# A batched matrix product on one core: the turns of loads and stores in its one DMA queue get unequal lengths

## The chip, the cores and the metric

The kernel runs on one core of a Trainium2 chip. The metric is device time in microseconds (us) of one execution; below it stands beside the span that the profile shows, which is about 1.8 us shorter. DMA is the moving of data between the chip's main memory (HBM) and the core's own. A transfer is issued when SyncE puts it in the queue, and has landed when the last of its 16 records in the trace, one for each DMA engine, is there.

## The reference

Sixteen independent products. Each takes x of 768 x 512 and y of 768 x 1024, both float32, and gives 512 x 1024 in float32:

```python
batch, m, k, n = 16, 512, 768, 1024
def reference(x, y):
    return np.einsum('bkm,bkn->bmn', x, y).astype(np.float32)
```

Per batch 1.57 MB of x and 3.15 MB of y are read, and 2.10 MB are written. I call x and y of one batch a pair. In all, 75.5 MB are read and 33.6 MB written.

## The kernel before

Every transfer is issued by the SyncE sequencer, into one queue, in the order of this program. Each load goes to one of two float32 buffers; VectorE casts it to bf16 (a 16-bit float); TensorE multiplies into PSUM, the memory for its results; ScalarE copies the result to one of five output buffers, which a store then empties.

```python
FIRST = 8
TURN = 4
NO = 5                                  # output buffers
...
def store(b):                           # may it be issued? not before the next batch's matmuls are done
    if b < B - 2:
        nc.sync.wait_ge(groups, 2 * (b + 2))
    else:
        nc.sync.wait_ge(outs, b - (B - 3))
    nc.sync.dma_start(o_v[b], ob[b % NO][:]).then_inc(so[b % NO], 16)

def load(b):                            # the buffer is free when the batch two before has been cast
    i = b % 2
    if b >= 2:
        nc.sync.wait_ge(cast, nx[b - 2])
    wide_dma("x", xs[i][:], x_v[b], 4, True).then_inc(sx[i], 16)
    ...
    wide_dma("y", ys[i][:], y_v[b], 2, True).then_inc(sy[i], 16)

for b in range(B):
    load(b)
    if b + 1 >= FIRST and (b + 1 - FIRST) % TURN == 0:
        a = b + 1 - FIRST
        for c in range(a, a + TURN):
            store(c)
for b in range(B - FIRST + TURN, B - 1):
    store(b)
...
for b in range(B):                      # ScalarE
    if b >= NO:
        nc.scalar.wait_ge(so[b % NO], 16 * (b // NO))     # the store from this buffer has landed
    ...
for b in range(B - NO, B - 2):          # SyncE, before the last store
    nc.sync.wait_ge(so[b % NO], 16 * (b // NO + 1))
...
nc.sync.dma_start(o_v[B - 1], ob[(B - 1) % NO][:])
```

So the queue holds 8 pairs, 4 stores, 4 pairs, 4 stores, 4 pairs, 8 stores. I call each such run a turn, and the passage from one to the next a switch.

## Time and profile before

| | before |
|---|---|
| time, median of the first 3 runs | 260.7 us |
| span of the profiled run | 258.8 us |
| busy: TensorE, VectorE, ScalarE | 70%, 32%, 24% |
| DMA queue, share of 16 engines | 98.6% |
| ScalarE waiting for stores | 60.1 us |

Busy shares of engines are means over the span, so a low share doesn't say that an engine is never waited for.

### The profile page before, as it was taken

Reading aid. Unit: us, or ns where it says so; the run is one execution under the profiler, and the core shown is the slowest. Engines: PE = TensorE matmul, PEld = TensorE weight load, DVE = VectorE, ACT = ScalarE, POOL = GpSimd, SP = SyncE. Lnnn points to the kernel's source line nnn. Section 1 sums busy time; section 2 is a strip of 40 time slices with the busy share of each in tenths; the row PEclk is TensorE's granted clock in tenths of the full one; section 3 lists DMA queues with packets and bytes.
Section 4 is the critical chain, followed back from the end, with each engine's and each line's share of the span. In section 5 each row is a group of like instructions: output and inputs, shape, how many; then the busy total and the mean of one; then the engine's idle time right before and its main releaser. Section 6 shows DMA issues by size and latency. Waiting matters only on the chain. (4 is left out here: it accounts for less than half of the span.)

```text
span 258.8 us, 2506 instructions
## 1 busy us (share of the span) xinstructions
PE 181.6 (70%) x768; PEld 89.3 (34%) x768; DVE 82.0 (32%) x33; ACT 60.9 (24%) x33; POOL 0.2 (0%) x4
## 2 busy tenths in 40 slices
PE   0009999999999006999499920899669980099950
PEld 0004555554545002454145500355325530035520
DVE  0261645527164350011734525002255262300000
ACT  1000442234220005222214002324402200413430
POOL 0000000000000000000000000000000000000000
PEclk9999999999999855899779985699979995569995
DMA  7999989899999999999999989999899999999987
GB/s 273 424 475 410 471 380 479 372 479 395 456 410 441 387 418 430 466 446 418 433 433 425 471 352 443 420 461 479 372 479 403 448 410 390 433 438 420 436 357 324
DMA packets 4514, 109.07 MB, mean 421 GB/s; under 512 B 768, under 2 KB 768, under 8 KB 768
## 3 DMA queue, kind: packets, MB, share of 16 engines
q1 hardware_dynamic: 4512, 109.05, 98.6%
q14 instruction: 2, 0.02, 0.0%
HBM read 75.50 MB, written 33.55 MB: 421 GB/s over the span
## 5 line engine op out<-in xcount | busy, mean ns | idle before, releaser
L157 PE MATMUL ps<-yb,xb 128*128 x768 | 181.6, 402 | 68.0 <-PEq L152 68.0
L157 PEld LDWEIGHTS ps<-yb,xb 128*128 x768 | 89.3, 116 | 159.8 <-issue 89.8
L173 ACT COPY ob<-ps 128x2048 f32<-128x2048 f32 x32 | 59.6, 1872 | 185.3 <-PE ps L157 125.2
L135 DVE CAST yb<-ys 128x6144 bf16<-128x6144 f32 (+1 forms) x17 | 53.8, 3172 | 77.8 <-DMA ys<-in_y_dram 77.8
L131 DVE CAST xb<-xs 128x3072 bf16<-128x3072 f32 x16 | 28.2, 1761 | 62.5 <-DMA xs<-in_x_dram 48.7
L173 ACT ACT_TABLE_LOAD x1 | 1.3, 1283 | 5.3 <-issue 5.3
L203 POOL MEMSET const-bfloat16-1.0<- 128x1 bf16 x1 | 0.1, 103 | 0.0
L203 POOL MEMSET const-uint8-127<- 128x1 uint8 x1 | 0.1, 102 | 0.0
L203 POOL MEMSET const-float32-0.0<- 128x1 f32 x1 | 0.1, 100 | 0.2 <-issue 0.2
L203 POOL MEMSET const-float32-1.0<- 128x1 f32 x1 | 0.1, 99 | 0.0
## 6 DMA issues: line engine op xcount, KB each, us to landing
ys<-in_y_dram SPq DMA_DIRECT2D x16, 3072.0 KB, 18.6
out_dram<-ob SPq DMA_DIRECT2D x16, 2048.0 KB, 27.2
xs<-in_x_dram SPq DMA_DIRECT2D x16, 1536.0 KB, 20.1
```

Source lines behind the costliest of these rows:

```text
L131: nc.vector.tensor_copy(xb[:, i], xs[i][:]).then_inc(cast, 1)
L135: nc.vector.tensor_copy(yb[:, i, ks], ys[i][:, ks]).then_inc(cast, 1)
L157: mm = nc.tensor.matmul(ps[g][:, m, nt], x_w[:, bass.ds(s, 1), kt, mo], yb[:, bass.ds(s, 1), kt, nt * NF:(nt + 1) * NF], start=(kt == 0), ...
L173: cp = nc.scalar.copy(ob[b % NO][:, g * HB:(g + 1) * HB].rearrange("p m (t f) -> p m t f", f=NF), ps[g][:])
L203: nc = _bacc.Bacc("TRN2", target_bir_lowering=False, num_devices=1)
```

## The change

The intent: let output buffers come free before ScalarE asks for them, and shorten the run of stores at the end, without changing how often the queue goes from loads to stores.

```diff
-    FIRST = 8
-    TURN = 4
+    TURNS = [(8, 5), (4, 4), (4, 7)]
...
-    for b in range(B):
-        load(b)
-        if b + 1 >= FIRST and (b + 1 - FIRST) % TURN == 0:
-            a = b + 1 - FIRST
-            for c in range(a, a + TURN):
-                store(c)
-    for b in range(B - FIRST + TURN, B - 1):
-        store(b)
+    loads, stores = iter(range(B)), iter(range(B - 1))
+    for nl, ns in TURNS:
+        for b in islice(loads, nl):
+            load(b)
+        for b in islice(stores, ns):
+            store(b)
```

The third turn takes stores 9 to 14; the last store, of batch 15, follows it, which makes seven.

More of the change, by code (lines that the diff above doesn't have):

```diff
@@ L6 @@
 from contextlib import ExitStack
+from itertools import islice
 import concourse.bass as bass
```

## The prediction

> **What bounds the kernel now.** I read the page from the top. Part 1 shows that no engine is near full: the tensor engine is busy for 70% of the span, the vector engine for 32%, the scalar engine for 24%. Parts 2 and 3 show what is full.
>
> ```profile
> span 258.8 us, 2506 instructions
> PE 181.6 (70%) x768; PEld 89.3 (34%) x768; DVE 82.0 (32%) x33; ACT 60.9 (24%) x33; POOL 0.2 (0%) x4
> ...
> DMA  7999989899999999999999989999899999999987
> ...
> q1 hardware_dynamic: 4512, 109.05, 98.6%
> ...
> HBM read 75.50 MB, written 33.55 MB: 421 GB/s over the span
> ```
>
> The reader is to see that one DMA queue carries every byte, and that its packets fill 98.6% of the time of all 16 engines. The small remainder lies at the two ends: in the stretches from the span's start, nothing moves before 1 us, and nothing after 257 us.
>
> The page's chain that ended last covers only 10% of the span (matmuls, then one copy), because it stops at an instruction whose releaser it cannot follow. So I do not take it as the bound. I go to the order of time on the vector engine, where each cast of y begins when its load lands.
>
> ```profile
> 80.94 3.36 DVE L135 CAST yb<-ys 128x6144 bf16<-128x6144 f32 x1 [5.47 <-DMA ys<-in_y_dram]
> 84.70 1.76 DVE L131 CAST xb<-xs 128x3072 bf16<-128x3072 f32 x1 [0.40 <-DMA xs<-in_x_dram]
> 92.12 3.36 DVE L135 CAST yb<-ys 128x6144 bf16<-128x6144 f32 x1 [5.66 <-DMA ys<-in_y_dram]
> 115.34 1.76 DVE L131 CAST xb<-xs 128x3072 bf16<-128x3072 f32 x1 [19.86 <-DMA xs<-in_x_dram]
> 122.58 3.36 DVE L135 CAST yb<-ys 128x6144 bf16<-128x6144 f32 x1 [5.48 <-DMA ys<-in_y_dram]
> 133.58 3.36 DVE L135 CAST yb<-ys 128x6144 bf16<-128x6144 f32 x1 [5.48 <-DMA ys<-in_y_dram]
> ```
>
> Within a turn of loads, y lands every 11.0 us (133.58 - 122.58), whatever the engines do. I call x and y of one batch, 4.72 MB, a pair: 4.72 MB in 11.0 us is 429 GB/s. Between y of batch 7 (92.12) and y of batch 8 (122.58) lie four stores and one pair: 30.46 - 11.0 = 19.46 us, so 4.87 us for a store of 2.10 MB, or 431 GB/s. A switch between loads and stores is included in that, and stores in the last turn, where there is no switch back, take the same.
>
> The scalar engine shows the same from the other side: its copy into a used output buffer waits for the store from it.
>
> ```profile
> 97.00 3.64 ACT L173 COPY ob<-ps 128x2048 f32<-128x2048 f32 x2 [21.69 <-DMA out_dram<-ob]
> 160.43 3.64 ACT L173 COPY ob<-ps 128x2048 f32<-128x2048 f32 x2 [18.55 <-DMA out_dram<-ob]
> 223.74 3.63 ACT L173 COPY ob<-ps 128x2048 f32<-128x2048 f32 x2 [19.83 <-DMA out_dram<-ob]
> ```
>
> These are stores 0, 4 and 8, each the first of its turn, landing 4.88, 4.88 and 4.89 us after the last y of the turn before it (92.12, 155.55, 218.85). The first store after a switch costs no more than any other. Adding up: first y lands at 14.98; 15 pairs at 11.0 are 165.0; 16 stores at 4.87 are 77.9; together 257.9. The last issue, at 251.67, takes 6.3 us to land, which is 258.0. The time is the sum of the transfers, in any order, with nothing left over.
>
> [...] y of batch 7 is issued at 73.35, and lands at 92.12, in the order of its issue. [...] after an idle stretch the granted clock was 0.50 from 89 to 105 us, and 96 matmuls took 23.85 us. I take 13.4 us for a batch begun cold (10.4 plus about 3) and 10.5 for a warm one; both are estimates from these rows.
>
> **The change part by part.** Instructions on the four compute engines are the same in kind, number and order; only the DMA-issuing engine has another order. It **removes** no transfer and **adds** none. It **moves** store 4 from the head of the second turn of stores to the end of the first, and store 8 from the head of the third to the end of the second. The numbers of switches are unchanged: three from loads to stores, two back. By the sums above the direct cost is 0 us.
>
> What else it could change is whether the queue runs dry. I worked through the new order with the durations above.
>
> Turn 1. Y of batch 7 lands at 92.1, and stores 0 to 4 at 97.0, 101.9, 106.7, 111.6, 116.5. Store 4 is issued when batch 5's matmuls are done (84.4: 73.84 + 10.55), and loads 8 follow at once, the casts that they wait for ending at 75.5 and 84.3. The queue then holds 8 us of load and 24 us of stores, so this wait of the issuer is hidden.
>
> Turn 2. X and y of batch 8 land at 120.2 and 127.4; y of 9, 10, 11 at 138.4, 149.4, 160.4. Batch 8 runs cold from 130.8 to 144.2, batch 9 to 154.6, batch 10 to about 165. Store 8 has to wait for batch 9, so it and loads 12 behind it are issued at about 155, when the queue still holds the rest of pair 11 and three stores (5.4 + 14.6 = 20 us). Hidden. Stores 5 to 8 land at 165.3 to 179.9.
>
> Turn 3. Y of 12 to 15 lands at 190.9, 201.9, 212.9 and 223.9, later than before by one store (5 us); the last stores are then 7 instead of 8, so 5 us are given back exactly. Batch 14's matmuls end at about 228.5; its copy waits for store 9 (228.7) and ends at 232.4; batch 15 runs from 230.8 to some 241 to 244; its last copy ends by about 246, where before it ended at 251.48 (249.61 + 1.87). So the **compute tail** is 5 us earlier. That is the intent, I think: output buffers come free before they are asked for, and the scalar engine's wait for stores falls from 60.1 us to about 22 + 5 + 4 = 31.
>
> What does that buy at the end? Before, the last store was issued only at 251.67.
>
> ```profile
> 250.00:251.50 1.50, 0.00 (x0) 0.00 (x0) 0.00 (x0) 1.48 (x1) 0.00 (x0) 1.00 0.72 306
> 251.50:253.00 1.50, 0.00 (x0) 0.00 (x0) 0.00 (x0) 0.00 (x0) 0.00 (x0) 0.65 0.46 197
> 253.00:257.00 4.00, 0.00 (x0) 0.00 (x0) 0.00 (x0) 0.00 (x0) 0.00 (x0) 0.50 1.08 459
> ```
>
> The columns at the end are granted clock, DMA share and GB/s. The missing shares are 0.28 x 1.5 + 0.54 x 1.5 = 1.23 us of the mean engine: a real hole. But the end is set by the slowest of the 16, not by the mean. Store 14, issued at 241.18, took 11.8 us to landing, thus 253.0; the last one landed at 258.0. That is 5.0 us apart against 4.87 for a store without a hole, so the slowest engine lost only about 0.15 us; the others idled because they had finished their shares early. After the change the last store is held only until store 13 lands (a wait on its semaphore precedes it; 253.0 - 4.9 = about 248), is issued near 248.3, and the hole closes. **Sum:** 0 for transfers, -0.15 for the hole, so 260.7 - 0.15 = about 260.5 us.
>
> **Rivals.** First, **the whole hole counts**: if all engines had been equally late, closing it gives 1.2 us, about 259.5. For it: 1.23 us is really missing. Against it: the 5.0 us between the last two landings. Still within 2%. Second, **long bursts of stores are slower**, or a switch from five stores back to loads costs more: each 1% on a store is 0.05 us, and 16 stores give 0.8 us, about 261.4. Against it: in the kernel before, stores run eight in a row at the end at the same 4.87. Third, **a new wait starves the queue**: store 4 or store 8 blocks the issuer while it waits for matmuls, and the loads behind it are held. If the tensor engine were 20 us later in turn 2 than I find, the queue would run dry by that excess; 5 us of it would make 265.5. Against it: a reserve of 20 us at the tighter place. Fourth, **the compute wait was the bound**: a reader of part 1 who sees 125.2 us of waiting on ACT and 68 us of idle PE may expect 5 us from the earlier compute tail, about 255.7. Against it: the transfers alone add up to 257.9 of 258.8.
>
> **Range and chances.** The centre is 260.5. The lower edge, 259.6, takes in most of the first rival; the upper one, 261.3, takes in the second and a few tenths of difference between chips (the three runs of before span 0.34 us). 2% is 5.2 us, so faster would need the fourth rival and slower the third: 1% and 2%.
>
> **What would show it.** Right: DMA share again near 98.6% or a little above; y of batch 8 landing at about 127.4 and of batch 15 at about 223.9; ACT's wait for stores near 31 us in place of 60.1; the last copy ending by about 246; the last store issued near 248 and no stretch with a share under 0.7 between 250 and 254; the span within 0.5 us of 258.8. Wrong: a hole in the DMA share in the stretches 115 to 125, 155 to 185 or 218 to 230, stores of over 4.95 us in the runs of five or seven, or a last store that is still issued after 251 us.

The clock and the 23.85 us are measured. The rates of 429 and 431 GB/s are measured, but that they leave no room was not shown. That only an empty queue costs time was the assumption. The 13.4 us for a cold batch is an estimate from the trace: two batches of 48 matmuls took 23.85 us, less 10.5 for the second.

## The result

The changed kernel took 260.72 us (median of 4 runs, 260.52 to 260.85); the kernel before, in 4 runs, 260.6 (260.4 to 260.74). The ratio is 1.0004, with a 95% interval from 0.9987 to 1.0022: no difference. The profiled span was 259.0 us, and each instruction kept its place on the four compute engines.

From the page of the changed kernel, in the order of the lines shown for the kernel before:

```profile
span 259.0 us, 2506 instructions
PE 179.0 (69%) x768; PEld 88.9 (34%) x768; DVE 82.0 (32%) x33; ACT 60.9 (24%) x33; POOL 0.2 (0%) x4
...
DMA  7999989899999999999999998999999999999995
...
q1 hardware_dynamic: 4512, 109.05, 98.5%
```

The queue is as full as before. From the timeline of the vector engine (start, duration, engine, line, operation; in brackets the idle time before it and what ended it), the casts that begin when y lands:

```profile
81.01 3.36 DVE L132 CAST yb<-ys 128x6144 bf16<-128x6144 f32 x1 [5.47 <-DMA ys<-in_y_dram]
...
92.25 3.36 DVE L132 CAST yb<-ys 128x6144 bf16<-128x6144 f32 x1 [5.71 <-DMA ys<-in_y_dram]
...
127.56 3.36 DVE L132 CAST yb<-ys 128x6144 bf16<-128x6144 f32 x1 [5.47 <-DMA ys<-in_y_dram]
...
223.98 3.43 DVE L132 CAST yb<-ys 128x3072 bf16<-128x3072 f32 x2 [3.51 <-DMA ys<-in_y_dram]
```

Between y of batch 7 (92.25) and y of batch 8 (127.56) lie five stores and a pair now: 35.31 - 11.0 = 24.3, or 4.86 us for a store. Y of batch 15 lands 5.1 us later than before (218.85), and one store fewer follows it. By the landing records the seven stores of the last turn took 4.84 to 4.99 us, 4.89 on average.

From the timeline of the scalar engine, the copies that waited for a store, and its last copy:

```profile
97.14 3.63 ACT L170 COPY ob<-ps 128x2048 f32<-128x2048 f32 x2 [21.76 <-DMA out_dram<-ob]
...
165.45 3.64 ACT L170 COPY ob<-ps 128x2048 f32<-128x2048 f32 x2 [9.01 <-DMA out_dram<-ob]
...
228.87 3.64 ACT L170 COPY ob<-ps 128x2048 f32<-128x2048 f32 x2 [8.28 <-DMA out_dram<-ob]
...
243.33 1.87 ACT L170 COPY ob<-ps 128x2048 f32<-128x2048 f32 x1 [3.26 <-PE ps L154]
```

The wait for stores fell from 60.1 to 39.1 us, and the last copy ends at 245.2 us instead of 251.5. Compute finishes over 6 us earlier, and the time doesn't move. The end of the queue, in the stretches of the view by windows (after the engines: granted clock, DMA share, GB/s):

```profile
250.00:251.50 1.50, 0.00 (x0) 0.00 (x0) 0.00 (x0) 0.00 (x0) 0.00 (x0) 0.50 0.97 415
251.50:253.00 1.50, 0.00 (x0) 0.00 (x0) 0.00 (x0) 0.00 (x0) 0.00 (x0) 0.50 1.07 459
253.00:257.00 4.00, 0.00 (x0) 0.00 (x0) 0.00 (x0) 0.00 (x0) 0.00 (x0) 0.50 0.77 328
```

The hole of 1.23 us that the mean DMA engine had between 250 and 253 is gone. In its place the last 4 us are at 0.77 instead of 1.08: the mean engine now finishes early, and the end waits for the slowest. The last store is issued at 249.08 and takes 9.1 us to land, at 258.2; before, it landed at 258.0.

The trace holds 16 landing records for each transfer, one for each DMA engine. From first to last they lie 1.44 us apart for store 9 before and 1.74 after; for store 14, 1.65 before and 2.03 after. For the last store itself it was 0.20 before, since the hole let the slow engines catch up with the others, and 2.03 after. I call this distance the **spread**; it returns in the experiments. Most of it belongs to two engines: at store 14 of the changed kernel 14 records lie within 0.94 us of the first, the other two 1.72 and 2.03 after it.

### The profile page after: what moved, and what is told of

It reads as the page before. It is cut to its first block, busy times and chain, and to the rows that moved or that the text cites. A ratio compares the mean times of both kernels' runs of the same rounds, so it can differ in the third digit from the quotient of the medians. Undisturbed runs are those within 1.5% of the kernel's fastest.

```text
span 259.0 us, 2506 instructions
## 1 busy us (share of the span) xinstructions
PE 179.0 (69%) x768; PEld 88.9 (34%) x768; DVE 82.0 (32%) x33; ACT 60.9 (24%) x33; POOL 0.2 (0%) x4
## 5 line engine op out<-in xcount | busy, mean ns | idle before, releaser
L154 PE MATMUL ps<-yb,xb 128*128 x768 | 179.0, 397 | 64.3 <-PEq L149 64.3
```

Source lines behind the costliest of these rows:

```text
L154: mm = nc.tensor.matmul(ps[g][:, m, nt], x_w[:, bass.ds(s, 1), kt, mo], yb[:, bass.ds(s, 1), kt, nt * NF:(nt + 1) * NF], start=(kt == 0), ...
```

## The experiments

My theory: the time is the sum of the transfers on the slowest DMA engine, whatever their order, as long as the queue never runs dry; a wait counts only as far as it runs dry. The main rivals: that the compute engines or their waits are part of the time; that the hole of the kernel before counted in full; that the length or the number of turns matters by itself. All experiments are edits of the changed kernel. The table counts the store of batch 15, which stands outside `TURNS`, in the last turn.

| run | turns: loads, stores ... | time us | ratio to before |
|---|---|---|---|
| the change | 8,5 4,4 4,7 | 260.72 | 1.0004 |
| e1_part | 8,5 4,3 4,8 | 260.93 | 1.0006 |
| e2_late | 8,3 4,4 4,9 | 264.74 | 1.0161 |
| e3_gate | as the change | 262.86 | 1.0082 |
| e4_alternate | 6,1 ten times 1,1, then 5 | 262.13 | 1.0057 |
| e5_block | 3,1 5,4 4,4 4,7 | 268.80 | 1.0306 |
| e6_long | 10,5 4,5 2,6 | 262.18 | 1.0071 |
| e7_less_matmul | as the change | 260.03 | 0.9980 |
| e8_half_stores | as the change | 251.05 | 0.9632 |
| e9_nine | 9,5 4,5 3,6 | 260.87 | 1.0006 |
| e10_pairs | 6,2 four times 2,2 2,6 | 261.57 | 1.0035 |
| e11_alternate_less | as e4_alternate | 262.65 | 1.0057 |

At the limit of 2% only e5_block is slower and e8_half_stores faster; all the others are the same. Where I read a smaller difference as real below, the 95% interval of its ratio doesn't hold 1; for e1_part and e9_nine it does.

### Is the time the sum of the transfers? (e7, e8)

```diff
 # e7_less_matmul
-                for kt in range(KT):
+                for kt in (0, KH):
-                            start=(kt == 0), stop=(kt == KT - 1))
+                            start=(kt == 0), stop=(kt == KH))
```

> The changed kernel with one third of its matmuls (two of six slices of the contraction; the result is wrong on purpose). My theory (the tensor engine is not on the path that sets the end): the tensor engine's busy time falls from 179 to about 60 to 70 us and the time stays at 260.7, within 0.4. Rival (waits of engines for matmuls, 140 us in the changed kernel's profile, are part of the time): several us faster.

The result is wrong, as meant. From its page:

```profile
PE 93.0 (36%) x256; PEld 34.2 (13%) x256; DVE 82.0 (32%) x33; ACT 60.5 (23%) x33; POOL 0.2 (0%) x4
```

TensorE lost half of its busy time (not two thirds; its granted clock was 0.69, against 0.88 in the changed kernel), and the kernel took 260.03 us. The ratio of 0.9980 has an interval of 0.9964 to 0.9997, so it is a little faster, by about 0.5 us against 86 us less of matmul. TensorE is not on the path that sets the end. The small rest I come back to.

```diff
 # e8_half_stores
-        nc.sync.dma_start(o_v[b], ob[b % NO][:]).then_inc(so[b % NO], 16)
+        h = HB if b in (4, 5, 6, 7) else MT
+        nc.sync.dma_start(o_v[b][:, :h], ob[b % NO][:, :h]).then_inc(so[b % NO], 16)
```

> The changed kernel with stores 4 to 7 writing half of their rows (wrong on purpose), so 4.19 MB of 109.05 MB less in the queue and nothing else changed. My theory (the time is the sum of the transfers): 4 x 4.87 / 2 = 9.7 us faster, near 251.0. Rival (compute and its waits would take over as the bound): less than that, under 5 us.

```profile
q1 hardware_dynamic: 4512, 104.86, 98.4%
```

251.05 us: 9.7 us less than the changed kernel, for 4.19 MB less, just what 4 x 4.87 / 2 gives. In this run the bytes taken from the queue came off the time one for one.

### What does the end cost? (e1, e2, e3)

```diff
 # e1_part
-    TURNS = [(8, 5), (4, 4), (4, 7)]
+    TURNS = [(8, 5), (4, 3), (4, 8)]
```

> One part of the change alone: store 4 goes to the first turn, but store 8 stays at the head of the last one (turns of stores 5, 3, 8). My theory (the time is the sum of the transfers, whatever their order, as long as the queue does not run dry): same time as both kernels, within 0.4 us of 260.7; the last turn is that of the kernel before, so the last store is again issued near 251.7 us and the hole of about 1.2 us in the mean DMA share near 251 to 253 us comes back without moving the end. Rival (the hole counts as a whole for the end, and the change merely lost as much elsewhere): about 1 us slower than the changed kernel.

260.93 us, ratio 1.0006. Store 4 alone moved: no difference either. The last store was issued at 251.21, nearly as late as before (251.67), and the shares show a smaller hole (0.11 x 1.5 + 0.15 x 1.5 = 0.39 us of the mean engine, not 1.2):

```profile
250.00:251.50 1.50, 0.00 (x0) 0.00 (x0) 0.00 (x0) 1.02 (x1) 0.00 (x0) 1.00 0.89 382
251.50:253.00 1.50, 0.00 (x0) 0.00 (x0) 0.00 (x0) 0.00 (x0) 0.00 (x0) 1.00 0.85 360
```

The spread of the last store was 1.19 us, that of store 14 2.21. The part of the expectation about the hole's size missed; the time did not.

```diff
 # e2_late
-    TURNS = [(8, 5), (4, 4), (4, 7)]
+    TURNS = [(8, 3), (4, 4), (4, 8)]
```

> The change turned round: turns of stores 3, 4, 9, so the last turn is two stores longer than after the change and one longer than before. Y of batch 15 should land at 214.1 us, store 7 at 219.0; batches 13, 14 and 15 follow it on the tensor engine (about 221 to 253), and the last store is issued near 254.8 us, while store 14 ends its data at about 252. My theory (compute tail is free until the last issue comes later than the end of the queue, and then counts one for one): end at 254.8 + 6.3 = 261.1 us in the span, thus about 3 us slower, near 263.6. Rival (the compute tail never matters, only the transfers do): 260.7. Rival (each turn's length matters by itself): no number.

264.74 us: 4.0 slower than before by the medians, where I had expected 2.9. The direction is that of the theory. The last copy on ScalarE and the last issue of SyncE:

```profile
253.62 1.86 ACT L170 COPY ob<-ps 128x2048 f32<-128x2048 f32 x1 [3.26 <-PE ps L154]
```

```profile
255.68 0.33 SPq L185 DMA_DIRECT2D out_dram<-ob  x1
```

It landed 6.3 us later, at 262.0, and the queue was dry more than once:

```profile
240.00:245.00 5.00, 5.00 (x24) 2.60 (x23) 0.00 (x0) 1.74 (x2) 0.00 (x0) 1.00 0.59 252
...
250.00:256.00 6.00, 3.59 (x17) 1.67 (x15) 0.00 (x0) 2.23 (x2) 0.00 (x0) 1.00 0.62 262
```

I had found the second hole and overlooked the first, in which store 13 waits for the matmuls of batch 14. Compute was 0.9 us later than I had worked out, which explains most of the miss: the end follows the last issue, at 6.3 us.

```diff
 # e3_gate
-    for b in range(B - NO, B - 2):
+    for b in range(B - NO, B - 1):
```

> The changed kernel, with the last store issued only when store 14 has landed (the wait before it takes in one store more). That takes the reserve away on purpose: store 14 lands at 253.3 us, the last is issued at about 253.6 and lands 6.3 us later at 259.9 instead of 258.2. My theory: 1.7 us slower than the changed kernel, near 262.4 us. Rival (issuing early never mattered, the latency is hidden in some other way): the same 260.7.

262.86 us, 2.1 slower than the changed kernel (expected 1.7). The last store was issued at 253.81 and took 6.3 us to land; before its data the queue was empty:

```profile
253.81 0.33 SPq L185 DMA_DIRECT2D out_dram<-ob  x1
```

```profile
253.00:254.00 1.00, 0.00 (x0) 0.00 (x0) 0.00 (x0) 0.00 (x0) 0.00 (x0) 0.50 0.00 0
254.00:255.00 1.00, 0.00 (x0) 0.00 (x0) 0.00 (x0) 0.00 (x0) 0.00 (x0) 0.50 0.62 262
```

So the last issue may come at 249.1 (the change), 251.2 (e1_part) or 251.7 (before) without harm, and costs 2 us at 253.8, though the only edit is one more wait. The kernel before stood near the edge. The change bought 2.6 us of reserve, which nothing in the kernel spends.

### What does a wait in the issuer cost? (e5)

```diff
 # e5_block
-    TURNS = [(8, 5), (4, 4), (4, 7)]
+    TURNS = [(3, 1), (5, 4), (4, 4), (4, 6)]
```

> The changed kernel, but store 0 goes early: 3 batches of loads, store 0, 5 batches of loads, stores 1 to 4, the rest as in the change. Store 0 waits for the matmuls of batch 1 (done at 42 us), and blocks the issuer, so loads 3 are held; y of batch 2 has landed at 37. My theory (a wait in the issuer counts as far as the queue runs dry): store 0 lands at 42.0 + 6.3 = 48.3 instead of 37.0 + 4.9 = 41.9, and all that follows is 6.4 us later: about 267.1 us, over 2% slower. Rival (later slack in the schedule takes it up, because the tensor engine is only 69% busy): under 262.

268.80 us, 3.1% slower. Store 0 was issued at 42.05 and the loads behind it were held:

```profile
34.00:36.00 2.00, 2.00 (x11) 1.02 (x9) 0.00 (x0) 0.00 (x0) 0.00 (x0) 1.00 0.52 221
36.00:38.00 2.00, 2.00 (x11) 1.05 (x10) 1.04 (x1) 1.13 (x1) 0.00 (x0) 1.00 0.00 0
38.00:40.00 2.00, 2.00 (x11) 1.07 (x10) 2.00 (x1) 0.76 (x1) 0.00 (x0) 1.00 0.00 0
40.00:42.00 2.00, 2.00 (x11) 1.04 (x10) 0.32 (x1) 0.00 (x0) 0.00 (x0) 1.00 0.00 0
```

By its landing records store 0 landed 12.4 us after y of batch 2, not 4.9: a loss of 7.5 at this place, of 8.1 in the whole time (there is also one turn more, which matters below). No later slack gave any of it back. My 6.4 was low by 1 us because the store took 7.3 us from issue to landing, not 6.3. So a store issued into an empty queue landed 6.3 us (e2_late, e3_gate) or 7.3 us (e5_block) after its issue, against 4.87 us for each store in a stream.

### Do length and number of turns matter by themselves? (e4, e6, e9, e10, e11)

```diff
 # e6_long
-    TURNS = [(8, 5), (4, 4), (4, 7)]
+    TURNS = [(10, 5), (4, 5), (2, 5)]
```

> More of the same: turns of loads 10, 4, 2 and of stores 5, 5, 6. As many switches. The queue should not run dry: the tightest place is load 15, which needs the cast of x of batch 13, which needs the matmuls of batch 11, about 203 us, when stores and pair 14 are queued until about 217. My theory (order is free): 260.7, within 0.4. Rival (the length of turns matters): longer turns would differ by more than that, in either direction.

262.18 us: I was wrong here, by 1.5 us. The tight place was not load 15 but load 10: its x waited for the cast of batch 8, which waited for matmuls that waited for ScalarE, which waited for store 0. It was issued here:

```profile
135.73 0.48 SPq L74 DMA_DIRECT2D xs<-in_x_dram  x1
```

By the landing records store 4 landed at 138.02 and this x at 143.03, 5.0 us later; a load of x that follows a store in the queue without a gap lands 3.6 to 3.7 later. That is a loss of 1.3 us. Whether it was this or the length of the turns, a turn shorter by one pair tells:

```diff
 # e9_nine
-    TURNS = [(8, 5), (4, 4), (4, 7)]
+    TURNS = [(9, 5), (4, 5), (3, 5)]
```

> Turns of loads 9, 4, 3 and of stores 5, 5, 5 with the last store on its own: nearly those of e6_long (10, 4, 2), which was 1.4 us slower, but the first load after the first turn of stores is now x of batch 9, which needs the cast of batch 7 (done at 86 us), and not x of batch 10, which needed the cast of batch 8, held by matmuls that waited for store 0. In e6_long that x was issued at 135.73, within 1 us of the end of the queue, and landed 5.0 us after the last store instead of 3.7. Theory A (e6_long was slower because the queue ran dry there): this one takes 260.7, within 0.5, and the load after store 4 lands 3.7 us after it. Theory B (longer turns are themselves slower): about 261.5 to 262, as e6_long.

260.87 us, ratio 1.0006: as theory A has it. The first x after store 4 was already in the queue,

```profile
87.28 0.48 SPq L74 DMA_DIRECT2D xs<-in_x_dram  x1
```

and landed 3.65 us after that store. Turns of 9 are as good as turns of 8; turns of 10 let the queue run dry.

```diff
 # e4_alternate
-    TURNS = [(8, 5), (4, 4), (4, 7)]
+    TURNS = [(6, 1)] + 10 * [(1, 1)] + [(0, 4)]
```

> Turns of one: 6 batches of loads, then store, load, store, load, and so on, then the last stores. 11 switches from loads to stores and 10 back, where both kernels have 3 and 2. The queue should never run dry, as each store waits for matmuls that are done some 10 us before its place in the queue. My theory (switches are free and order is free): 260.7, within 0.5. Rival (a switch from loads to stores costs some 0.2 us, as y of batch 7, the last load before the first switch, lands 11.2 us after the one before it rather than 11.0): 8 more switches of 0.2 make 1.6 us, near 262.3.

262.13 us, 1.5 slower than before by the ratio: the rival's number, not mine. From the vector engine's timeline, y of successive batches, with one store and one switch each way between them:

```profile
117.99 3.36 DVE L132 CAST yb<-ys 128x6144 bf16<-128x6144 f32 x1 [5.46 <-DMA ys<-in_y_dram]
134.05 3.36 DVE L132 CAST yb<-ys 128x6144 bf16<-128x6144 f32 x1 [5.71 <-DMA ys<-in_y_dram]
150.55 3.36 DVE L132 CAST yb<-ys 128x6144 bf16<-128x6144 f32 x1 [6.10 <-DMA ys<-in_y_dram]
166.80 3.36 DVE L132 CAST yb<-ys 128x6144 bf16<-128x6144 f32 x1 [5.88 <-DMA ys<-in_y_dram]
182.63 3.36 DVE L132 CAST yb<-ys 128x6144 bf16<-128x6144 f32 x1 [5.49 <-DMA ys<-in_y_dram]
```

The steps are 16.06, 16.50, 16.25 and 15.83, where a pair and a store make 11.0 + 4.87 = 15.87. So three of these four steps cost 0.2 to 0.6 us. The six other steps of this kind in the run, from y of batch 5 on, are 15.83 to 15.99, so most cost next to nothing. The spread grew from 0.99 at y of batch 1 to 2.92 at the last store, while the first engine to land lost little: the first landing of store 14 came at 251.39 here and at 251.33 in the kernel before. Switches set back a few engines, not all: 13 of the 16 records of store 14 lie within 1.33 us of the first, the other three 2.12 to 3.02 after it. Nor was the queue ever short: from y of batch 2 to store 14 each transfer was issued at least 10.1 us before the first landing of the one ahead of it.

```diff
 # e10_pairs
-    TURNS = [(8, 5), (4, 4), (4, 7)]
+    TURNS = [(6, 2)] + 4 * [(2, 2)] + [(2, 5)]
```

> Turns of two: 6 loads, then 2 stores, 2 loads and so on; 6 switches from loads to stores where both kernels have 3, and e4_alternate, which was 1.4 us slower, has 11. Theory A (each such switch sets the slowest DMA engine back by about 0.17 us, 1.4 / 8): 260.7 + 3 x 0.17 = 261.2. Theory B (e4_alternate lost its time in some other way, in a few places where turns of one leave the queue short): 260.7.

261.57 us, ratio 1.0035 with an interval of 1.0022 to 1.0049: 0.9 us slower for three switches more, about 0.3 each. Between turns of one and the kernel before, it is what theory A expects in direction, and nearly double in size.

```diff
 # e11_alternate_less
-    TURNS = [(8, 5), (4, 4), (4, 7)]
+    TURNS = [(6, 1)] + 10 * [(1, 1)] + [(0, 4)]
-                for kt in range(KT):
+                for kt in (0, KH):
-                            start=(kt == 0), stop=(kt == KT - 1))
+                            start=(kt == 0), stop=(kt == KH))
```

> The turns of one of e4_alternate, with one third of the matmuls as in e7_less_matmul (wrong on purpose). e7_less_matmul took 260.0. Theory A (the switches themselves cost 1.4 us): 260.0 + 1.4 = 261.4. Theory B (the setback of the slowest engine at switches comes from what the compute engines do beside it, or from a queue kept short by matmuls): about 260.0 to 260.4.

262.65 us by the median, with one run of four at 261.24; the ratio is 1.0057. Against e7_less_matmul (0.9980) that is 0.77%, or 2.0 us for 8 more switches, 0.25 each, where theory A expected 1.4; the two intervals (1.0033 to 1.0080, 0.9964 to 0.9997) lie apart, but leave the size open between some 0.9 and 3 us. With a third of the matmuls the loss at switches stays, so it is not a queue kept short by matmuls; here too each transfer up to store 14 was issued at least 10 us ahead. Theory A holds in direction: a turn more costs 0.2 to 0.3 us here, unevenly.

**What stays open.** Why the slowest engine is set back at some switches and not at others, and which of the 16 it is: the records that I read carry no number for it. The packets in the trace show part of it. A load's packet of 49,152 bytes takes 1.83 us as a rule. After the first 18 us, 48 of them in e4_alternate and 59 in e11_alternate_less took over 5% longer, up to 2.69 us, against 7 before and 8 after the change; of these, 45, 53, and all 7 and 8 ran beside a store's packet on another engine, so at a switch. But of the 379 load packets of e4_alternate that ran beside a store, 334 were not slowed. Nor are switches the only occasion: in e3_gate stores 9 to 12 took 4.94 to 5.00 us and stores 13 and 14 took 4.87 and 4.84, with one switch before the first of them and none after, while in e7_less_matmul stores 9 to 15 took 4.82 to 4.89. That may be the 0.5 us by which e7_less_matmul was faster, so something that goes with matmuls may be part of it; no run shows what.

No experiment points to a version that beats both kernels. A version with two turns of stores was not built. Loading the last batches in one turn needs the matmuls of batch 11, and those wait for store 5, so store 5 would have to go into the first turn, where its issue waits for the matmuls of batch 6. Whether that gains or loses, no run shows.

## Why the prediction was right

- **The bound** (the time is the sum of the transfers): shown. Half stores took off exactly their bytes, 9.7 us (e8), two thirds of the matmuls next to nothing, 0.5 us (e7), and a queue that ran dry showed up in full (2.1 us in e3; 7.5 us at the place and 8.1 in the time in e5; 1.3 and 1.5 in e6).
- **The direct cost of the change, 0 us**: shown. Five stores in a row took 4.86 us each, as four did; e1_part and e9_nine, with other lengths, took the same time.
- **The new order worked out turn by turn**: y of batches 8 and 15 came at 127.56 and 223.98 (127.4 and 223.9 predicted), the last copy ended at 245.2 (by 246), the last store was issued at 249.08 (248.3), and no stretch from 250 to 254 was under a share of 0.7. The waits of stores 4 and 8 in the issuer were hidden. One sign of being wrong did appear, once: store 12 took 4.99 us, over the limit of 4.95, though the seven stores of its turn took 4.89 on average.
- **The scalar engine's wait for stores** was 39.1 us, not 31. The terms for batches 10 and 14 were 9.0 and 8.3, not 5 and 4: I counted from the end of the matmuls that fill PSUM, and the profile counts from the end of the copy before. It had no effect on the time.
- **-0.15 us for the hole**: not to be seen in the total, which no run could show so small. In the trace the last store landed 4.84 us after store 14 instead of 5.03, so the term itself, 0.19 us, was there. But store 14 landed 0.37 us later than before (253.35 against 252.98), by setbacks of the slowest engine along the way, which the prediction didn't have, so the end came 0.17 us later and not earlier. These are figures of one profiled run each, within the scatter of the runs; that the centre of 260.5 lay as close as 0.2 us is in part luck. The argument that the slowest engine sets the end, not the mean, is the one that held: the whole hole closed, and 1.2 us didn't come.
- **The rivals**: the first (the hole counts in full) falls with the result; the second (long bursts) falls with the 4.86 us of the five stores and with e9_nine (its 261.4 should have read 261.3: 260.5 + 0.8); the third (starving) did happen in e5_block, at a price of 8.1 us, but the change doesn't trigger it; the fourth (compute waits as the bound) falls with e7.
- **The step that was too simple** is "the first store after a switch costs no more than any other". The store doesn't, but the load before the switch can: y of batch 7 lands 11.18 us after y of batch 6 in the prediction's own lines (92.12 - 80.94), where 11.0 is the rule. For the same reason "in any order, with nothing left over" holds only for as many turns. Runs e4, e10 and e11 put the price at 0.2 to 0.3 us for each extra turn. As the change keeps the number of turns, it didn't matter.

## What to carry to other kernels

Here one queue was full to 98.6%, and its transfers added up to 257.9 us of a span of 258.8. The reordering of this change moved the time by 0.1 us, and a compute tail that ended 6 us earlier only bought reserve. So when a queue looks like this, add up its transfers first. What reordering did in other runs is harm (4.0 us in e2_late, 8.1 in e5_block): find the place where an issue comes latest against the end of the queue, by following all waits back (store to copy to matmul to cast to load), and issue well before the transfer ahead of it lands: 4.3 us before was enough for the last store of the changed kernel, and even 2.5 in e1_part, while 2.3 us before was too late for a load in e6_long. And look at the slowest DMA engine rather than the mean share before counting a hole as lost time: here a hole of 1.23 us of the mean engine closed, and the last landing came 0.17 us later.
